# Gelu of the state-space output: on ScalarE at the end of each branch, in token order, instead of in pieces over three engines inside the attention

## The chip, the cores and the metric

One core of a Trainium2 chip runs the whole kernel. Its engines are TensorE (PE), VectorE (DVE), ScalarE (ACT), GpSimd (POOL) and SyncE (SP, which issues most of the DMAs). The metric is the device time of one execution in microseconds; of a kernel the median of several runs is given.

## What is computed

One decoder block on 1024 tokens of width 1024, 16 meta tokens ahead of them (1040 rows). An input projection gives the state-space input `u` (512 wide), q, k, v and two gates. The change touches the state-space mixer's output: an S5 scan for 32 groups of 16 channels, a gelu, and a gated linear unit. Cut from the reference:

```python
def s5_mixer(u, ...):
    ...                                   # complex diagonal scan, states s_re, s_im
    y = (jnp.einsum('blgp,gcp->blgc', s_re, c_re) - jnp.einsum('blgp,gcp->blgc', s_im, c_im)
         + d * ug)
    y = jax.nn.gelu(y.reshape(bsz, seq_len, SSM_WIDTH)).astype(u.dtype)
    return y * jax.nn.sigmoid(y @ glu_w + glu_b)

def reference(...):
    ...
    y_ssm = s5_mixer(u, ...)
    o = diff_attention(q, k, v, lam, slopes)
    mixed = sigmoid(g_ssm) * (y_ssm @ w_ssm_out) + sigmoid(g_att) * (y_att @ w_att_out)
    h = h + mixed @ w_o
    h = h + conv_glu_ffn(rmsnorm(h, norm2_g), w_up, conv_w, conv_b, w_down)
```

## The kernel before

All activations lie with channels on the 128 partitions and tokens along the free dimension. Matmuls are made exact enough by splitting each operand into a rounded part and a rest (`whi`, `wlo` of a weight, `yhi`, `ylo` of y), so that each product is three matmuls; a split is a copy on ACT and a subtract on DVE or, from the fourth gate on, a subtract on POOL.

**State-space part** (about 60 to 280 us). The 512 channels are four branches of 128. Each goes through inflow, scan, back and outflow; `ssm` is a generator that yields between the steps, and other projections are placed between them. The outflow's matmuls go to PSUM, ACT copies them to SBUF (`Vs<-yps`), and one DMA writes them to DRAM as `d_y[b]`. In this form the partitions hold position-within-a-chunk and channel, and the free dimension group and chunk: not token order. The tail of this part, from 232 us, has the last branch's steps with the first gate projections (`PRE`) between them.

**Attention** (about 290 to 640 us). Scores of a block are computed in two or three pieces of up to 512 columns: PE makes two matmuls (lines 1419 and 1420), DVE adds the bias, takes the row maximum and moves the piece to SBUF (line 1421), then a negated maximum `nm`, an exponential on ACT (`S<-S,nm`), a combination of the two softmaxes on DVE (`S<-S,c`), a transpose on PE (`wt`) copied back by ACT, and the product with v (`po`). Score pieces rotate through few PSUM tiles, so PE's next piece needs DVE to have emptied an earlier one. PE's gaps between these are filled by a generator `fillers`: first the 16 gate projections (`gates`, each three tiles of 48 matmuls, evicted by DVE as `gate<-ps_mm,R`, a tanh on ACT, then a store to `d_gate[i]` by SP), then the state-space glu and its output projection (`glu_and_out`). PE's order in the attention is the program's; the order on the other engines is made by a scheduler from its own estimate of times.

**The gelu.** When gate 14 is begun (`YGATE`), `load_y` reads the four branches back from `d_y` with 32 DMAs of 65 KB on SP, in pieces of 520 bytes, into four tiles `yt` of 128 x 8 x 130 (position in chunk, chunk). The gelu is in eight pieces of 128 x 520: the square on POOL, two multiply-adds on DVE and a tanh on ACT between them; the result is twice the gelu. During gate 15, after every sixth filler step, `split_y` splits one `yt` into `yhi` (ACT) and `ylo` (DVE), with a factor 0.5, and turns it into token order by a strided write. In `glu_and_out`, the multiply-add with `yt` reads it strided, and the split takes a factor 0.25.

**Buffers.** The tiles `gate`, `yt`, `y2`, `u` and several others share one tag `t` of five buffers: whoever takes a buffer waits for the last reader of the tile that had it.

## Time and profile before

| | us |
|---|---|
| median of three runs | 1437.9 (1436.21, 1437.9, 1437.98) |
| the profiled execution | 1438.99 |
| its span in the profile | 1437.2 |
| PE busy | 1407.9 (98%) |
| DVE busy | 1051.0 (73%) |
| ACT busy | 630.8 (44%) |
| POOL busy | 379.7 (26%) |
| granted clock of PE, mean | 0.993 |

Times in the views are counted from the span's start. A timeline's row gives start, length, engine, line, operation, output and input tile, and in brackets how long the engine had been idle before it and what ended that. `s` is a PSUM tile of scores, `S` its copy in SBUF, `ps_mm` a PSUM tile of a projection. The granted clock of a stretch is 1.00 at 2.4 GHz and 0.50 at 1.2 GHz. The line numbers are those of the kernel before; in the changed one, line 1421 is line 1429, and 446 is 452.

### The profile page before, as it was taken

Reading aid. Unit: us, or ns where it says so; the run is one execution under the profiler, and the core shown is the slowest. Engines: PE = TensorE matmul, PEld = TensorE weight load, DVE = VectorE, ACT = ScalarE, POOL = GpSimd, SP = SyncE. Lnnn points to the kernel's source line nnn. Section 1 sums busy time; section 2 is a strip of 40 time slices with the busy share of each in tenths; the row PEclk is TensorE's granted clock in tenths of the full one; section 3 lists DMA queues with packets and bytes.
Section 4 is the critical chain, followed back from the end, with each engine's and each line's share of the span. In section 5 each row is a group of like instructions: output and inputs, shape, how many; then the busy total and the mean of one; then the engine's idle time right before and its main releaser. Section 6 shows DMA issues by size and latency. Waiting matters only on the chain.

```text
span 1437.2 us, 22951 instructions
## 1 busy us (share of the span) xinstructions
PE 1407.9 (98%) x8714; PEld 1298.4 (90%) x8714; DVE 1051.0 (73%) x2030; ACT 630.8 (44%) x1180; POOL 379.7 (26%) x250
## 2 busy tenths in 40 slices
PE   8999999999998999999999999999999999999998
PEld 7999999999998999889998999988889997788887
DVE  7999996345646978548366998888766769896574
ACT  6255554345544766433254543333333333444442
POOL 2000000121111311000221156766655567131030
PEclk9999999999999999999999999999999999999999
DMA  5433343362434425656433223333323337944331
GB/s 199 137 76 115 105 122 98 111 189 60 116 102 109 115 75 185 197 191 220 133 132 114 93 81 125 126 125 117 111 97 110 111 110 258 360 150 154 123 119 58
DMA packets 93053, 191.45 MB, mean 133 GB/s; under 512 B 27536, under 2 KB 36880, under 8 KB 92944
## 3 DMA queue, kind: packets, MB, share of 16 engines
q1 hardware_dynamic: 92944, 190.00, 41.0%
q8 instruction: 68, 1.11, 0.3%
q14 instruction: 41, 0.34, 0.1%
HBM read 133.28 MB, written 55.50 MB: 131 GB/s over the span
## 4 chain that ended last, share of the span: by engine, by line
PE 76%; DVE 10%; DMA 5%; POOL 4%; issue 3%; ACT 2%; SPq 1%; DVEq 0%; ACTq 0%; POOLq 0%
PE ps_mm L184 38%; PE ps_mm L132 28%; PE po L1455 3%; DMA wraw<-in_w_up 2%; DVE wop L94 2%; POOL crow L94 2%; DVE crow L103 1%; PE s L1419 1%; PE wt L1464 1%; PE s L1420 1%; PE qss L371 1%; POOL S L94 1%; DVE u L94 1%; DMA wd<-in_w_down 1%; DMA yt<-d_y 1%
## 5 line engine op out<-in xcount | busy, mean ns | idle before, releaser
L132 PE MATMUL ps_mm<-B,wop 128*128 128x512 f32 (+2 forms) x2772 | 436.6, 319 | 4.3 <-DVE u L94 3.4
L132 PEld LDWEIGHTS ps_mm<-B,wop 128*128 128x128 f32 x2772 | 395.2, 189 | 45.3 <-ACT wop L106 5.2
L184 PE MATMUL ps_mm<-bop,wop 128*128 128x512 f32 x924 | 216.0, 395 | 2.6 <-DVE bop L94 2.6
L184 PEld LDWEIGHTS ps_mm<-bop,wop 128*128 128x128 f32 x924 | 174.1, 189 | 44.4 <-DVE bop L94 3.5
L184 PE MATMUL ps_mm<-hhi,whi 128*128 128x342 f32 (+2 forms) x432 | 138.0, 330 | 1.9 <-ACT hhi L106 1.9
L184 PE MATMUL ps_mm<-hlo,whi 128*128 128x342 f32 (+2 forms) x432 | 139.6, 323 | 0.1
L184 PE MATMUL ps_mm<-hhi,wlo 128*128 128x342 f32 (+2 forms) x432 | 139.5, 324 | 0.0
L106 ACT ACTIVATE whi<-wraw 128x1024 fp32r<-128x1024 f32 (+3 forms) x62 | 62.1, 1003 | 133.2 <-PE ps_mm L184 53.6
L94 DVE TENSOR_TENSOR wop<-wraw,wop 128x512 fp32r<-128x512 f32 x88 | 98.0, 1119 | 23.6 <-ACT wop L106 23.2
L132 PE MATMUL ps_mm<-hhi,whi 128*128 128x348 f32 (+3 forms) x336 | 111.9, 333 | 0.2 <-ACT rms_u L106 0.2
L132 PE MATMUL ps_mm<-hhi,wlo 128*128 128x348 f32 (+3 forms) x336 | 109.7, 326 | 0.0
L132 PE MATMUL ps_mm<-hlo,whi 128*128 128x348 f32 (+3 forms) x336 | 108.8, 324 | 0.0
L94 POOL TENSOR_TENSOR wlo<-wraw,whi 128x1024 fp32r<-128x1024 f32 x18 | 44.6, 2477 | 214.1 <-ACT whi L106 211.9
L94 DVE TENSOR_TENSOR wop<-S,wop 128x512 fp32r<-128x512 f32 x66 | 64.9, 983 | 48.1 <-ACT wop L106 48.1
L106 ACT ACTIVATE bop<-act 128x512 fp32r<-128x512 f32 x77 | 48.4, 632 | 117.3 <-PE ps_mm L184 117.3
L1421 DVE CUSTOM_DVE_ANT_0 S<-s,bias 128x348 f32<-128x348 f32 (+9 forms) x120 | 57.7, 483 | 56.6 <-PE s L1420 56.0
L94 POOL TENSOR_TENSOR crow<-crow,T 128x512 f32<-128x512 f32 x44 | 70.6, 1618 | 96.3 <-DVE T L94 90.8
L106 ACT ACTIVATE wop<-wraw 128x512 fp32r<-128x512 f32 x88 | 54.1, 626 | 93.2 <-DMA wraw<-in_w_up 51.6
L94 DVE TENSOR_TENSOR bop<-act,bop 128x512 fp32r<-128x512 f32 x77 | 60.1, 781 | 44.0 <-ACT bop L106 43.9
L106 ACT ACTIVATE wop<-S 128x512 fp32r<-128x512 f32 x66 | 40.4, 626 | 109.5 <-POOL S L94 98.8
L184 PEld LDWEIGHTS ps_mm<-hhi,whi 128*128 128x128 f32 x432 | 81.2, 190 | 3.1 <-ACT hhi L106 2.5
L184 PEld LDWEIGHTS ps_mm<-hlo,whi 128*128 128x128 f32 x432 | 83.0, 192 | 0.8 <-DVE hlo L103 0.6
(317 smaller groups left out, 3055.6 us busy)
## 6 DMA issues: line engine op xcount, KB each, us to landing
wraw<-in_w_up SPq DMA_DIRECT2D x49, 512.0 KB, 3.6
wraw<-in_w_in SPq DMA_DIRECT2D x30, 512.0 KB, 4.4
d_act<-crow SPq DMA_DIRECT2D x22, 512.0 KB, 2.9
act<-d_act SPq DMA_DIRECT2D x44, 256.0 KB, 3.7
wd<-in_w_down SPq DMA_DIRECT2D x22, 512.0 KB, 7.3
d_t<-T SPq DMA_DIRECT2D x33, 256.0 KB, 4.1
act<-d_t SPq DMA_DIRECT2D x33, 256.0 KB, 3.1
d_gate<-gate SPq DMA_DIRECT2D x16, 513.0 KB, 4.9
```

The source lines that it names most:

```text
L94: (eng or self.nc.vector).tensor_tensor(out=out, in0=in0, in1=in1, op=op)
L103: self.nc.vector.scalar_tensor_tensor(out=out, in0=in0, scalar=s, in1=in1, op0=op0, op1=op1)
L106: self.nc.scalar.activation(out, in_, func, **kw)
L132: self.nc.tensor.matmul(out=ps, lhsT=w, rhs=b, start=(i == 0), stop=(i == n - 1))
L184: self.nc.tensor.matmul(out=ps, lhsT=w, rhs=b, start=first and i == 0, stop=last and i == 2)
L371: self.nc.tensor.matmul(out=ps, lhsT=self.blk, rhs=v, start=True, stop=True)
L1419: nc.tensor.matmul(out=ps, lhsT=q, rhs=self.KH[j][:, c0m:c0m + cm], start=True, stop=False)
L1420: nc.tensor.matmul(out=ps, lhsT=q, rhs=self.KL[j][:, c0m:c0m + cm], start=False, stop=True)
L1421: nc.vector.tensor_tensor_reduce(out=s[0:M, c0:c0 + cn], in0=ps[0:M, off:off + cn], in1=self.bias[0:M, b0 + c0:b0 + c0 + cn], scale=1.0, s ...
L1455: nc.tensor.matmul(out=po[0:M], lhsT=l, rhs=rr, start=(kk == 0), stop=(kk == nb))
L1464: nc.tensor.transpose(ps[:, r], w[:, NM + 128 * kk:NM + 128 * (kk + 1)], b.ident)
```

## The change

Branch 3's gelu is made by the outflow's evictions on ACT (the function Gelu in place of Copy), so `d_y[3]` holds the gelu already. For branches 0 to 2, `load_branch` reads `d_y` back in the tail of the state-space part (24 small DMAs on SP), `gelu_y` makes one activation of 128 x 8 x 130 on ACT with a strided write into token order, and ACT's own queue stores it to a new `d_g[i]`. The table with Gelu (and Tanh) is loaded by a pinned preload in that tail; before, the table with Tanh was loaded just ahead of the first gate's tanh. The exponential's table is loaded once more ahead of the attention's first exponential. `load_y` then reads three contiguous tiles of 128 x 1040 from `d_g`, and branch 3 raw, which ACT copies into token order. The split of y is contiguous and without a factor (so a plain subtract on DVE), the multiply-add of the glu is contiguous, and the factor behind it is 0.5.

```diff
--- before.py
+++ after.py
@@ -47,7 +47,7 @@
 YGATE = 14
 GAP_V = 1.5
 NEWTON, NORM_SCALE = (1.0, -2.0, 16.0), -8192.0
-GELU_CUTS = 2
+GELU = "gelu_apprx_tanh_and_others"
 LN_EXP = "natural_log_exp_and_others"
 TCARGS = {"schedule_with_timeline_sim": True}
 
@@ -211,6 +211,7 @@
             self.d_gate = [d(f"d_gate{i}", [128, T2]) for i in range(16)]
             self.d_u = [d(f"d_u{i}", [GB, 16, CH, NJ]) for i in range(4)]
             self.d_y = [d(f"d_y{i}", [CH, 16, GB, NJ]) for i in range(4)]
+            self.d_g = [d(f"d_g{i}", [128, T]) for i in range(3)]
             self.d_m1 = [d(f"d_m1{i}", [128, T2]) for i in range(8)]
             self.d_o = [d(f"d_o{i}", [128, T2]) for i in range(H)]
             self.d_h2 = [d(f"d_h2{i}", [128, SEQ]) for i in range(8)]
@@ -238,7 +239,12 @@
                 step(1)
                 self.v_block(h)
             fill = self.fillers()
-            for _ in ssm:
+            tc.keep_in_program_order(nc.scalar.preload_act_table_set(GELU))
+            loaded = []
+            for n, _ in enumerate(ssm):
+                for z in loaded:
+                    self.gelu_y(*z)
+                loaded = [(i, self.load_branch(i)) for i in ((0, 1), (2,), ())[min(n, 2)]]
                 spent = 0.0
                 while spent < PRE:
                     spent += next(fill)
@@ -729,7 +735,7 @@
                                          rhs=d["Vv"][:, g0 + g], start=True, stop=False))
                     nc.tensor.matmul(out=ps[:, g], lhsT=toe[:, g0 + g].rearrange("p n c -> p (n c)"),
                                      rhs=u[:, g0 + g], start=False, stop=True)
-                self.act(y[:, g0:g0 + ng], ps, AF.Copy)
+                self.act(y[:, g0:g0 + ng], ps, AF.Copy if b < 3 else AF.Gelu_apprx_tanh)
             nc.sync.dma_start(out=self.d_y[b].rearrange("n c g j -> (n c) g j"), in_=y)
             self.tap(f"y{b}", y.rearrange("p g j -> p (g j)"))
             st[b] = None
@@ -770,27 +776,30 @@
     def load_y(self):
         self.yt, self.yh, self.yl = [], [], []
         for i in range(4):
-            t = self.tmp.tile([128, CH, NJ], F32, tag="t", name="yt")
-            for g in range(GB):
-                self.nc.sync.dma_start(out=t[g * 16:(g + 1) * 16],
-                                       in_=self.d_y[i][:, :, g, :].rearrange("n c j -> c n j"))
+            t = self.row(name="yt")
+            if i < 3:
+                self.nc.sync.dma_start(out=t, in_=self.d_g[i])
+            else:
+                self.act(t.rearrange("p (j n) -> p n j", n=CH), self.load_branch(i), AF.Copy)
             self.yt.append(t)
 
-        z = self.rowp.tile([128, CH, NJ], F32, tag="R", name="yz")
-        n = CH // GELU_CUTS
-        for i in range(4 * GELU_CUTS):
-            y = self.yt[i // GELU_CUTS][:, i % GELU_CUTS * n:(i % GELU_CUTS + 1) * n]
-            t = z[:, i % GELU_CUTS * n:(i % GELU_CUTS + 1) * n]
-            self.tt(t, y, y, ALU.mult, eng=self.nc.gpsimd)
-            self.stt(t, t, 1 / 0.044715, y, ALU.add, ALU.mult)
-            self.act(t, t, AF.Tanh, scale=0.044715 * (2 / np.pi) ** 0.5)
-            self.stt(y, t, 1.0, y, ALU.add, ALU.mult)
+    def load_branch(self, i):
+        t = self.tmp.tile([128, CH, NJ], F32, tag="t", name="yraw")
+        for g in range(GB):
+            self.nc.sync.dma_start(out=t[g * 16:(g + 1) * 16], in_=self.d_y[i][:, :, g, :].rearrange("n c j -> c n j"))
+        return t
+
+    def gelu_y(self, i, t):
+
+        o = self.row(name="yg")
+        self.tc.keep_in_program_order(self.nc.scalar.activation(o.rearrange("p (j n) -> p n j", n=CH), t,
+                                                                AF.Gelu_apprx_tanh))
+        self.nc.scalar.dma_start(out=self.d_g[i], in_=o)
 
     def split_y(self, i):
         hi = self.A.tile([128, T], F32R, tag="A", name="yhi")
         lo = self.A.tile([128, T], F32R, tag="A", name="ylo")
-        pv = lambda z: z.rearrange("p (j n) -> p n j", n=CH)
-        self.split(self.yt[i], pv(hi), pv(lo), 0.5)
+        self.split(self.yt[i], hi, lo)
         self.yh.append(hi)
         self.yl.append(lo)
 
@@ -813,9 +822,8 @@
                                                                yh[k][:, cs], yl[k][:, cs]) for k in range(4)])])
                 th = y2[:, cs]
                 self.act(th, ps, AF.Tanh, scale=0.5, bias=self.glub[:, m:m + 1])
-                self.stt(th.rearrange("p (j n) -> p j n", n=CH), th.rearrange("p (j n) -> p j n", n=CH), 1.0,
-                         yt[m][:, :, c0 // CH:(c0 + cn) // CH].rearrange("p n j -> p j n"), ALU.add, ALU.mult)
-                self.split(th, hi[:, cs], lo[:, cs], 0.25)
+                self.stt(th, th, 1.0, yt[m][:, cs], ALU.add, ALU.mult)
+                self.split(th, hi[:, cs], lo[:, cs], 0.5)
             self.tap(f"y2{m}", y2[:, 8:])
             y2h.append(hi)
             y2l.append(lo)
```

PE's order is the same before and after. What moves on the other engines:

DVE, in the attention, from the eviction of a score piece (`S,m<-s,bias`) of the block whose scores run at 456 us before. Before, with the pieces of the gelu between the evictions:

```order
L1421 ISA S,m_5114<-s,bias 128x348
L1421 ISA m_5114 128x1
L103 SCALAR_TENSOR_TENSOR yz<-yz,yt 128x520
L1421 ISA S,m_5114<-s,bias 128x344
L1421 ISA m_5114 128x1
L103 SCALAR_TENSOR_TENSOR yz<-yz,yt 128x520
L1430 TENSOR_REDUCE nm<-m_5114 128x1
L103 SCALAR_TENSOR_TENSOR yt<-yz,yt 128x520
L1421 ISA S,m_5152<-s,bias 128x348
L1421 ISA m_5152 128x1
```

and now:

```order
L1429 ISA S,m_5154<-s,bias 128x348
L1429 ISA m_5154 128x1
L1429 ISA S,m_5154<-s,bias 128x344
L1429 ISA m_5154 128x1
L1438 TENSOR_REDUCE nm<-m_5154 128x1
L98 TENSOR_SCALAR nm<-nm 128x1
L1429 ISA S,m_5192<-s,bias 128x348
L1429 ISA m_5192 128x1
L1429 ISA S,m_5192<-s,bias 128x348
L1429 ISA m_5192 128x1
```

The pieces `yz` and `yt` are gone; the evictions of the score pieces follow one another, with the block's maximum between.

ACT, in the tail of the state-space part (`Vs<-Vv` is the swap after the last branch's scan, `gate` the tanh of the first two gates). Before:

```order
L106 ACTIVATE Vs<-Vv 64x4x129 x4
L106 ACT_TABLE_LOAD
L106 ACTIVATE gate<-gate 128x1026
L106 ACTIVATE whi<-wraw 128x1024
L106 ACTIVATE gate<-gate 128x1026
L106 ACTIVATE Vs<-yps 128x390 x2
```

and now:

```order
L106 ACTIVATE Vs<-Vv 64x4x129 x4
L795 ACTIVATE yg<-yraw 128x8x130
L106 ACTIVATE gate<-gate 128x1026
L797 DMA d_g_116<-yg 128x1040
L795 ACTIVATE yg<-yraw 128x8x130
L797 DMA d_g_117<-yg 128x1040
L795 ACTIVATE yg<-yraw 128x8x130
L106 ACTIVATE whi<-wraw 128x1024
L106 ACTIVATE gate<-gate 128x1026
L797 DMA d_g_118<-yg 128x1040
L106 ACTIVATE Vs<-yps 128x390 x2
```

Three gelus and three stores issued by ACT stand among the tanhs and the weight splits; the table load is no longer here but stands nine rows earlier, ahead of the copy `whi<-wraw` that stood at 240.78 us.

ACT, in the attention, from the split of a weight and the tanh of gate 13 on (`O`, `junk` take the attention's output from PSUM, `wt` copies transposed weights). Before:

```order
L106 ACTIVATE whi<-wraw 128x1024
L106 ACTIVATE gate<-gate 128x1026
L106 ACTIVATE yz<-yz 128x520
L106 ACTIVATE O<-po 128x128
L106 ACTIVATE junk,oss<-po 128x128
L106 ACTIVATE wt<-wt 128x512
L106 ACTIVATE yz<-yz 128x520
L106 ACTIVATE S,z_5263<-S,nm 128x1040
L106 ACTIVATE wt<-wt 16x128
L106 ACTIVATE yz<-yz 128x520
L106 ACTIVATE S,Z0s<-S,nm 128x144
L106 ACTIVATE yz<-yz 128x520
```

and now:

```order
L106 ACTIVATE whi<-wraw 128x1024
L106 ACTIVATE gate<-gate 128x1026
L106 ACTIVATE S,z_5251<-S,nm 128x1040
L106 ACTIVATE O<-po 128x128
L106 ACTIVATE junk,oss<-po 128x128
L106 ACTIVATE wt<-wt 128x512
L106 ACTIVATE wt<-wt 16x128
L106 ACTIVATE yt<-yraw 128x8x130
L106 ACTIVATE S,Z0s<-S,nm 128x144
L106 ACTIVATE S,z_5324<-S,nm 128x144
```

The pieces of the tanh `yz` are gone, and one copy `yt<-yraw` of branch 3 stands between the transposes' copies and the exponentials of the next block. Its target has the buffer that gate 13's tile had, and its source has the buffer that gate 14's tile gets; on DVE the first eviction of gate 14 (`gate<-ps_mm,R`) stands between the next block's scores:

```order
L103 SCALAR_TENSOR_TENSOR S<-S,c 128x1040
L1429 ISA S,m_5294<-s,bias 128x144
L1429 ISA m_5294 128x1
L98 TENSOR_SCALAR nm<-m_5294 128x1
L94 TENSOR_TENSOR gate<-ps_mm,R 128x342
L1429 ISA S,m_5309<-s,bias 128x144
L1429 ISA m_5309 128x1
L98 TENSOR_SCALAR nm<-m_5309 128x1
```

The strided `ylo` and glu multiply-adds keep their places on DVE, in contiguous form; POOL loses its eight squares.

## Rows read from the trace of the kernel before

**Rows 1.** The page: busy us (share of the span) xinstructions.
```profile
PE 1407.9 (98%) x8714; PEld 1298.4 (90%) x8714; DVE 1051.0 (73%) x2030; ACT 630.8 (44%) x1180; POOL 379.7 (26%) x250
```

**Rows 2.** PE's waits, 440 to 520: engine, line, releaser; us, times, longest.
```profile
PE s L1419 <- DVE m L1421: 4.1, 1, 4.1
PE ps_mm L184 <- DVE gate L94: 2.1, 1, 2.1
```

**Rows 3.** Stages: PE, PEld, DVE, ACT, POOL busy; clock, DMA, GB/s.
```profile
464.00:469.34 5.34, 5.34 (x19) 5.12 (x19) 5.34 (x14) 4.39 (x7) 3.40 (x3) 0.50 0.63 114
506.89:510.30 3.41, 3.41 (x14) 3.40 (x13) 0.95 (x3) 0.65 (x5) 1.13 (x1) 0.50 0.67 195
1014.00:1020.00 6.00, 4.57 (x29) 3.97 (x28) 3.90 (x9) 1.78 (x3) 4.22 (x3) 1.00 0.18 52
1227.10:1230.50 3.40, 3.40 (x8) 2.72 (x9) 3.40 (x5) 0.00 (x0) 1.06 (x1) 0.50 0.85 266
```

**Rows 4.** Timeline of PE, three places: start, length, [idle before <-releaser].
```profile
457.34 0.32 PE L1420 MATMUL s<-KL,QQ 128*128 128x344 f32 x1
...
1017.60 0.47 PE L132 MATMUL ps_mm<-B,wop 128*128 128x512 f32 x1 [1.43 <-DVE u L94]
...
1227.08 0.79 PE L184 MATMUL ps_mm<-bop,wop 128*128 128x512 f32 x1 [2.01 <-DVE bop L94]
```

**Rows 5.** Timeline of DVE behind its first wait for yt.
```profile
461.98 1.53 DVE L103 SCALAR_TENSOR_TENSOR yz<-yz,yt 128x520 f32<-128x520 f32 x1 [4.91 <-POOL yz L94]
463.43 0.50 DVE L1421 CUSTOM_DVE_ANT_0 S<-s,bias 128x344 f32<-128x344 f32 x1
```

**Rows 6.** Timeline of POOL, its first squares.
```profile
460.89 2.06 POOL L94 TENSOR_TENSOR yz<-yt 128x520 f32<-128x520 f32 x2 [7.95 <-DMA yt<-d_y]
```

**Rows 7.** Timeline of SP: issues of the yt loads.
```profile
451.34 15.82 SPq L775 DMA_DIRECT2D yt<-d_y  x25
```

**Rows 8.** Timeline of DVE, 490 to 506: ylo and the last gate's evictions.
```profile
493.10 6.64 DVE L103 SCALAR_TENSOR_TENSOR ylo<-yt,yhi 128x1040 fp32r<-128x1040 f32 x3
...
504.38 1.35 DVE L94 TENSOR_TENSOR gate<-ps_mm,R 128x342 f32<-128x342 f32 x3
```

**Rows 9.** Groups by shape: xcount | busy us, mean ns | idle before <-releaser.
```profile
L106 ACT ACTIVATE yhi<-yt 128x1040 fp32r<-128x1040 f32 x4 | 9.0, 2306 | 0.0
...
L106 ACT ACTIVATE crow<-crow 128x1024 f32<-128x1024 f32 x22 | 23.3, 1058 | 22.2 <-DVE crow L103 22.2
...
L94 DVE TENSOR_TENSOR wlo<-wraw,whi 128x1024 fp32r<-128x1024 f32 x38 | 46.3, 1219 | 7.5 <-ACT whi L106 7.5
...
L103 DVE SCALAR_TENSOR_TENSOR ylo<-yt,yhi 128x1040 fp32r<-128x1040 f32 x4 | 8.9, 2291 | 0.0
```

**Rows 10.** Timeline of ACT in the tail of the state-space part.
```profile
240.78 1.06 ACT L106 ACTIVATE whi<-wraw 128x1024 fp32r<-128x1024 f32 x1 [1.55 <-PE ps_mm L132]
...
257.65 1.28 ACT L106 ACT_TABLE_LOAD   x1
...
258.94 1.06 ACT L106 ACTIVATE gate<-gate 128x1026 f32<-128x1026 f32 x1
```

**Rows 11.** Timeline of DVE and PE there.
```profile
258.81 0.51 DVE L94 TENSOR_TENSOR gate<-ps_mm,R 128x342 f32<-128x342 f32 x1
...
269.02 0.32 PE L184 MATMUL ps_mm<-hhi,whi 128*128 128x342 f32 x1
...
273.75 0.38 PE L728 MATMUL yps<-Vv,CL 128*128 128x130 f32 x2
```

**Rows 12.** Timeline of ACT behind the attention's first exponential.
```profile
317.24 1.06 ACT L106 ACTIVATE whi<-wraw 128x1024 fp32r<-128x1024 f32 x1 [1.88 <-issue]
```

**Rows 13.** ACT's gate13 tanh; landing of d_gate stores; PE's score matmul near 478.
```profile
467.87 1.05 ACT L106 ACTIVATE gate<-gate 128x1026 f32<-128x1026 f32 x1
...
DMA to landing us min/median/max: 3.5/4.7/8.2
...
477.95 0.37 PE L1419 MATMUL s<-KH,QQ 128*128 128x456 f32 x1
```

## The prediction

> **What bounds the kernel now.** I read the page's busy line first: TensorE (PE) is busy 98% of the span, the vector engine (DVE) 73%, ScalarE (ACT) 44% [rows 1]. So work that leaves DVE, ACT or GpSimd (POOL) is worth nothing by itself; it pays only where PE stands still for it, or where PE runs slowly after it stood still. The second view is the list of what PE waited for in the attention stretch that holds the pieces of the gelu. It has two entries of size: 4.1 us for an attention score matmul that waits for DVE, and 2.1 us for a glu matmul that waits for the last gate's eviction on DVE [rows 2]. The third view is the stage table with the granted clock: behind each of these pauses a stretch stands at clock 0.50, the lower of the two levels (1.2 instead of 2.4 GHz). It lasts to 469.34 after the first and for 3.41 us after the second [rows 3]. The same happens behind the pause of 2.01 us before 1227.08, and does not behind the pause of 1.43 us before 1017.60 [rows 3, 4]. So I charge a new pause with a slow stretch where it is as long as those that had one (2.01 and more), and with none where it is as short as the one that had none.
>
> Then I follow each pause to its cause. **First pause.** DVE executes in order. It sat idle 4.91 us before its first piece of the gelu at 461.98, waiting for POOL's square [rows 5]; POOL had itself sat 7.95 us until 460.89, waiting for the load of yt [rows 6]; SP was busy for 15.82 us issuing 25 of the 32 small loads [rows 7]. The score eviction that PE needed stood behind that piece, and ran at 463.43 [rows 5]. PE restarted at 464.00, where the slow stretch of [rows 3] begins for it. **Second pause.** Four strided ylo of 2.29 us each stand on DVE [rows 9]; three took 493.10 to 499.74, and the gate's evictions came only at 504.38 [rows 8].
>
> What the two are worth, if they vanish entirely: 4.1 us of standing [rows 2], plus half of the 5.34 us that PE worked at half clock (464.00 to 469.34 [rows 3]), 2.7, is 6.8. Then 2.1 plus half of 3.41, 1.7, is 3.8. Together 10.6.
>
> **What the change removes there.** All eight squares on POOL and all sixteen DVE pieces, so nothing on DVE waits for yt any more before the score evictions. The score eviction that ran at 463.43 had its matmul done by 457.66 [rows 4], so DVE can run it then: the first pause goes completely, and with it the slow clock. Costs in its place: ACT now does S exp, weight split, gate tanh, and an output eviction with less spread. I allow 0.15 for a transpose's copy that comes late.
>
> For the second pause ylo becomes one contiguous subtract instead of a strided piece. The nearest row is the contiguous subtract of 128x1024, 1.219 us against 2.291 [rows 9]. Four of them save 4.3 us of DVE before the gate's evictions, where PE was missing 2.1, and the DVE time of the gelu pieces ahead of them has gone too. So some 2 us of slack are left and the 3.8 comes back. The strided multiply-adds of the glu get shorter as well, but no pause of any size hangs on them: nothing.
>
> **What the change adds, and what hides it.**
> (a) Branch 3's gelu rides on its outflow evictions in place of a copy: nothing, as a function's cost does not show in the rows (gelu in the feed-forward part, 128x1024, takes 1.058 [rows 9], gate tanh, 128x1026, 1.05 [rows 13]).
> (b) In the tail of the state-space part, 24 small loads on SP, three gelus on ACT, three stores issued from ACT's own queue. SP is moved first: eleven loads ahead of the Toeplitz loads, at some 0.6 us of issue each by 15.82/25 [rows 7], so these come about 7 us later; PE reads their tile only in the outflow that begins at 273.75 [rows 11], some 30 us on. Nothing. A strided gelu costs 2.31 us by the strided yhi, which is the nearest row, or 1.06 by the contiguous gelu [rows 9]; I take 2.31. ACT's queue by rows: the table load that stood at 257.65 [rows 10] is moved forward into idle time of 1.55 us before 240.78 [rows 10], where its 1.28 fits. The first gelu takes 257.65 to 259.96, gate0's tanh ends at 261.0, the second gelu at about 263.4 (a store's issue between them, 0 to 0.6). DVE's gate1 eviction at 258.81 [rows 11] writes the buffer that the second gelu reads, so it now waits till about 263.6, and what is queued behind it on DVE, the scan's product Vv, with it. PE wants the gate's tile in PSUM free at 269.02 and Vv at 273.75 [rows 11]: 5 us and more of cover. The third gelu waits for its loads and for the first store's landing, and is done by about 272.6; the weight split and gate1's tanh behind it come 7 us late, and no matmul before 290 uses those weights. Nothing again.
> (c) ACT's table must be changed back before the first exponential of the attention: one more load, 1.28 us by the row at 257.65. If it comes in whole behind the wait of that exponential, ACT still idles 1.88 us behind the exponential, before 317.24 [rows 12], which absorbs it. Nothing.
>
> The Trainium skill, page "ScalarE: Activation LUTs", section "What ACT_TABLE_LOAD costs", speaks against (c): a load costs about 1.28 us and a drain of about 1.38 with it, 2.66 for each change of set. In the trace the next activation starts at 258.94, 1.29 after the load's start, so the row carries the load and no drain behind it. By the page the exponential would start up to 2.66 us late, of which 1.88 is absorbed, and 0.8 would fall on the weight split at 317.24; the sum would not move by more than that.
>
> (d) **The new wait.** Branch 3's y is loaded raw and copied on ACT into token order, strided, 2.31 us by yhi [rows 9]. Its target buffer was that of gate13, so the copy must wait until gate13's store has landed. This is a wait that before did not have. Gate13's tanh ran at 467.87 [rows 13], 3.87 us after PE's restart, most of it at half clock. With PE running on from 459.86 at full clock I estimate the tanh at 462.1 and its store issued at 463.2. Stores of gates land 3.5 to 8.2 us after issue, median 4.7 [rows 13]: 467.9, at worst 471.4. ACT is blocked until then, with two exponentials of 128x144 and an output eviction queued behind the copy. DVE's first eviction of gate14 needs the raw buffer and waits for the copy's end, about 470.2; two score evictions stand behind it. PE's next score matmul (477.95 before [rows 13]; 477.95 − 6.8 = 471.15 now) needs the first of them: 470.2 + 0.5 for the gate eviction + 0.3 to 0.5 for the score eviction is 471.0 to 471.2. At the median landing the wait just touches PE, and the next score, 1.6 us on, some tenths more. Every us by which the landing is later costs PE one, and a long pause the slow clock as well. So 0 at the low end, 3.5 + 1.7 at the high end; I take 1.0, as the wait is nearest to the median row.
>
> **Sum.** 10.6 − 0.15 − 1.0 = 9.5 us. The profiled execution took 1438.99 (span 1437.2, so 1.8 lie around the span and do not change); its median sibling 1437.9. The sum comes from waits of one execution and I subtract it from the median: 1437.9 − 9.5 = 1428.4.
>
> **The rivals.**
> *The copy's wait grows to 2 us and more.* For it: the store's landing was 8.2 us once [rows 13], and two loads of q and k rows now stand directly ahead of it in SP's queue. Against: these loads are due long before 463. Price: 2.5 of pause + 1.7 of slow clock instead of 1.0, gain 6.4: 1431.5.
> *The second pause stays.* For it: the copy delays everything on DVE before the splits, and branch 3's split is the last of four. Against: 4.3 us less of ylo. Price: only the first pause pays, 6.8 − 1.15 = 5.65: 1432.3; half of it gone, about 1430.
> *The copy costs little.* If its strided write cost what the contiguous gelu costs, 1.058 us instead of 2.306 [rows 9], it would end 1.25 us earlier and PE would not wait: gain 10.5, 1427.4. Against: yhi is the same write, with another output type. The Trainium skill, same page and section, gives an activation 0.19 us plus 0.833 ns per element of a partition, 1.05 us for 1040, and names no layout; the contiguous row agrees, yhi does not, so I hold to yhi.
> *Nothing is gained.* DVE turns out to be late at 460 to 464 for another reason than the yt load, for instance as ACT's exponentials feed it late. Against: the score eviction has its input from 457.7 on, and DVE was idle. Price: 1437 to 1439.
> *Slower, by the state-space tail.* The second gelu holds DVE at gate1's first eviction. It decides from the point where that gelu ends after 268.5 (269.02 less an eviction of 0.5): each us beyond costs PE one, and a long pause another 1.7 for the clock. To eat the 9.5 and more it would have to end at 280, 16 us past my estimate; the gelus would have to take 10 us each, where no row shows more than 2.5 for one pass of 1040 elements on ACT, or the raw loads land 16 us late. Price: 1441 to 1444.
>
> **How the numbers follow.** Both pauses gone, with a wait at the copy of under 2 us: 0.60, of it 0.15 for the cheap copy; 1426.5 to 1429.4. Copy's wait of 2 us and more: 0.16, 1430 to 1432.5. Second pause stays or stays in part: 0.13, 1430 to 1432.3. Nothing gained: 0.05. Slower: 0.04. More than the two pauses (the small ones at 479, 489, 549 and 552, together 0.9, go too): 0.02, down to 1426.4. Bounds: gain 10.6 + 0.9 and a run 0.9 lower than the sum give 1425.5; the two rivals and a run 0.5 higher give 1432.8. Range 1425.5 to 1432.8. This kernel's measurement tells apart about 0.2%, 2.9 us: faster means under 1435.0, slower over 1440.8. Faster 0.91, same 0.05, slower 0.04.
>
> **What would show it.** In the waits of PE between 440 and 520 both entries should be gone, and the stage table should stand at clock 1.00 from 455 to 515. If a pause of PE stands near 471 to 473, with DVE's gate eviction behind ACT's copy, (d) is right, and its length gives the mis-sizing. ACT should show the copy with idle time ahead of it that ends with the landing of gate13's store. A strided gelu of 2.3 us near 258, DVE idle at gate1's first eviction until about 263.6, and no pause of PE from 255 to 280 confirm (b); a pause there is the slower case. A table load of 1.28 before the attention's first exponential and no pause after it confirm (c). The prediction is wrong if the clock is not 1.00 after 460 though no pause is left, or if a pause at 459.9 stays without any yt piece ahead of the score eviction.

## The result and the profile after

The changed kernel takes 1431.0 us (median of 5 runs, 1429.1 to 1434.1), against 1437.9 before. The ratio is 0.9949, with a 95% interval of 0.9931 to 0.9968: a gain of 7.3 us by that ratio, 4.6 to 9.9 by the interval. Measured once more in another session (a0 below) it is 0.9944 [0.9928, 0.9959]. The forecast was 1428.4 in a range of 1425.5 to 1432.8, and faster with 0.91. It is faster by over 0.2%, the time lies in the range, 2.6 us above the forecast.

The page's busy line of after, with the columns of [rows 1]:

```profile
PE 1404.2 (98%) x8714; PEld 1295.4 (91%) x8714; DVE 1029.2 (72%) x2014; ACT 631.9 (44%) x1177; POOL 371.8 (26%) x242
```

PE's busy share is 98% as before. Its busy time fell by 3.7 us, where the profiled span fell by 8.0 (1437.2 to 1429.2), so this line shows less than half of the gain. PE's waits show more: both entries of [rows 2] are gone in the stretch 440 to 520. What stands there instead is new.

```profile
PE s L1427 <- DVE m L1429: 1.1, 2, 0.6
```

To lay two kernels side by side I cut the stretch around the change at four instructions of PE that both have. The first cut is a matmul of a gate projection, 4.7 us ahead of the old first pause; the last is 150 us on, in the attention. The length of each piece is then the time from one instruction to the same instruction. The first two of the four pieces of before (columns as in [rows 3]: stretch, its length, busy us of PE, PEld, DVE, ACT, POOL, granted clock, DMA share, GB/s):

```profile
455.12:481.04 25.92, 21.68 (x123) 20.19 (x121) 19.84 (x46) 10.80 (x25) 12.05 (x9) 0.87 0.71 168
481.04:512.11 31.07, 28.67 (x180) 26.82 (x178) 25.56 (x56) 22.48 (x36) 5.55 (x5) 0.95 0.35 102
...
```

And of after, between the same instructions:

```profile
456.58:477.02 20.44, 19.33 (x123) 18.02 (x121) 10.70 (x41) 9.61 (x21) 2.37 (x1) 1.00 0.66 178
477.02:503.59 26.57, 26.57 (x179) 25.31 (x178) 17.38 (x45) 16.49 (x34) 6.31 (x4) 1.00 0.33 102
...
```

Piece 1 holds the old first pause and the new copy, piece 2 the old second pause. They are 5.5 and 4.5 us shorter and the clock stands at 1.00 in both, where before had 0.87 and 0.95. The four together went from 149.9 to 139.8: 10.1 us. The work that PE does is the same; what went is the standing still and the matmuls at half clock.

The same cut was made in every kernel. All lengths in us; "outside" is the span less the four pieces:

| kernel | piece 1 | piece 2 | piece 3 | piece 4 | sum | outside | median us | ratio to before [95%] |
|---|---|---|---|---|---|---|---|---|
| before | 25.92 | 31.07 | 72.91 | 20.01 | 149.9 | 1287.3 | 1437.9 | |
| b0 before, once more | 25.70 | 31.05 | 72.94 | 20.12 | 149.8 | 1290.1 | 1441.7, one run | |
| after | 20.44 | 26.57 | 72.11 | 20.69 | 139.8 | 1289.4 | 1431.0 | 0.9949 [0.9931, 0.9968] |
| a0 after, once more | 21.34 | 26.58 | 72.12 | 20.72 | 140.8 | 1287.6 | 1431.4 | 0.9944 [0.9928, 0.9959] |
| e1 contiguous copy | 20.27 | 26.58 | 72.61 | 20.24 | 139.7 | 1289.0 | 1430.5 | 0.9940 [0.9924, 0.9957] |
| e2 two copies | 22.09 | 26.58 | 72.13 | 22.37 | 143.2 | 1289.2 | 1434.8 | 0.9965 [0.9953, 0.9976] |
| e6 branch 3 early | 18.79 | 26.58 | 72.25 | 22.60 | 140.2 | 1290.9 | 1431.9 | 0.9945 [0.9927, 0.9963] |
| e3 strided split | 22.97 | 28.56 | 72.11 | 22.81 | 146.5 | 1290.3 | 1434.6 | 0.9957 [0.9940, 0.9974] |
| e7 no gelu pieces | 22.54 | 27.78 | 73.30 | 20.36 | 144.0 | 1289.3 | 1434.1 | 0.9963 [0.9950, 0.9975] |
| e4 four loads | 23.24 | 28.77 | 72.92 | 20.13 | 145.1 | 1286.3 | 1436.3 | 0.9979 [0.9965, 0.9992] |
| e5 three gelus | 20.87 | 26.58 | 72.11 | 22.59 | 142.2 | 1293.2 | 1435.8 | 0.9976 [0.9962, 0.9990] |
| e8 early and orow | 18.79 | 26.58 | 71.93 | 17.84 | 135.1 | 1294.6 | 1427.6 | 0.9920 [0.9901, 0.9938] |
| e9 orow alone | 21.32 | 26.58 | 72.12 | 17.60 | 137.6 | 1287.1 | 1427.0 | 0.9916 [0.9900, 0.9932] |

Two executions of one code differ by 0.1 to 1.0 us inside the four pieces and by 1.8 to 2.8 outside. So the pieces tell apart what the medians only bound. A profile is of one run, not of the median one: those of e3, e7 and e8 are of the slowest run of their kernel, that of e4 of the second fastest of ten. The ratios are to runs of before in the same session (a0, e1, e2 and e6 shared one; e3, e4 and e7 another; e5, e8 and e9 a third).

### The profile page after: what moved, and what is told of

Read it like the earlier page. It is cut to its first block, busy times and chain, and to the rows that moved or that the text cites. A ratio compares the mean times of both kernels' runs of the same rounds, so it can differ in the third digit from the quotient of the medians.

```text
span 1429.2 us, 22918 instructions
## 1 busy us (share of the span) xinstructions
PE 1404.2 (98%) x8714; PEld 1295.4 (91%) x8714; DVE 1029.2 (72%) x2014; ACT 631.9 (44%) x1177; POOL 371.8 (26%) x242
## 3 DMA queue, kind: packets, MB, share of 16 engines
q8 instruction: 68, 1.11, 0.3%
## 4 chain that ended last, share of the span: by engine, by line
PE 88%; DVE 6%; DMA 3%; issue 1%; ACT 1%; POOL 1%; SPq 0%; ACTq 0%; DVEq 0%; POOLq 0%
PE ps_mm L184 40%; PE ps_mm L132 37%; PE po L1463 3%; DVE wop L94 1%; PE s L1427 1%; PE wt L1472 1%; PE s L1428 1%; PE qss L377 1%; DMA wraw<-in_w_up 1%; DMA wd<-in_w_down 1%; PE vps L694 1%; PE yps L736 1%; PE yps L734 0%; PE km L672 0%; DVE crow L103 0%
```

## The experiments

Edits are against the changed kernel, or against before where that is said.

**The changed kernel once more (a0).** 

> The changed kernel once more, for its own spread and as the base of the others. By the sum of waits: both pauses of the kernel before gone, two pauses of together 1.1 us behind the copy of branch 3's y, and the rest of the 9.5 us lost elsewhere only by chance (the first 42 us of the profiled execution took 1.3 longer than before, ahead of anything that the change touches). Then the time is 1429 to 1431 and the pause of 1.87 us near 592 (0.60 before) is seen again or not by chance. Rival: the changed kernel is slower at the start or near 592 by its order; then both stand in this profile as well.

It measured 0.9944, as the first time. The copy waits for the store of gate13, and here the trace names it (ACT's timeline):

```profile
462.92 1.04 ACT L106 ACTIVATE gate<-gate 128x1026 f32<-128x1026 f32 x1
...
470.72 2.20 ACT L106 ACTIVATE yt<-yraw 128x1040 f32<-128x1040 f32 x1 [3.85 <-DMA d_gate<-gate]
```

PE's pauses behind it are 1.50 and 0.52 us, against 0.60 and 0.51 in the first profile of after. Nothing in the code differs; the landing was 1.0 us later after the store's issue (6.7 against 5.7).

**A cheaper copy (e1)**

```
-  self.act(t.rearrange("p (j n) -> p n j", n=CH), self.load_branch(i), AF.Copy)
+  self.act(t.rearrange("p (n j) -> p n j", n=CH), self.load_branch(i), AF.Copy)
```

> The changed kernel with the copy of branch 3's y written contiguously (so its glu input stands in the wrong token order). By my step (d): the copy takes about 1.06 instead of 2.25 us, the chain copy, gate eviction, score eviction ends 1.2 earlier, the two pauses near 473 and 475 (0.60 and 0.51) vanish, 0.9 to 1.1 us faster than the changed kernel. Rival (the layout does not set an activation's cost): the copy still takes 2.25 and nothing changes.

ACT's timeline of e1:

```profile
469.75 1.08 ACT L106 ACTIVATE yt<-yraw 128x1040 f32<-128x1040 f32 x1 [3.90 <-DMA d_gate<-gate]
```

The copy takes 1.08 instead of 2.25 us, so the layout of the write makes its price. Piece 1 is 0.2 to 1.1 us shorter than in the two runs of after, and pauses of 0.43 and 0.52 are left. The time, 0.9940, can't be told from a0. The store lands so late (6.5 us after its issue here) that even a copy of half the length touches PE.

**The copy twice (e2)**

```
-  self.act(t.rearrange("p (j n) -> p n j", n=CH), self.load_branch(i), AF.Copy)
+  raw = self.load_branch(i)
+  for _ in range(2):
+      self.act(t.rearrange("p (j n) -> p n j", n=CH), raw, AF.Copy)
```

> The changed kernel with that copy made twice, 2.25 us more on ACT. By my step (d) PE's pauses near 473 grow by 2.25, from 1.1 to about 3.4, and a stretch at half clock follows, 1.7 more: 3 to 4.5 us slower than the changed kernel. Rival (DVE and PE have cover there): under 1 us slower.

PE's timeline at the copy:

```profile
477.73 0.48 PE L1429 MATMUL s<-KH,QQ 128*128 128x456 f32 x1 [3.04 <-DVE m L1431]
```

And the stage behind it:

```profile
477.80:485.00 7.20, 7.20 (x46) 6.68 (x47) 5.80 (x24) 4.47 (x10) 0.11 (x1) 1.00 0.01 2
```

Counted from the first cut the copies end at 470.67 + 4.45 − 457.10 = 18.0, in a0 at 470.72 + 2.20 − 456.00 = 16.9. PE stands 3.04 us against 2.02 in a0. The copies end 1.1 us later and PE stands 1.0 us longer: the chain from landing over copy and gate eviction to the score is real. But no half clock follows a pause of 3.04 us. The median is 3.3 us above a0's; 0.75 of it stands in piece 1 of the profiles and 1.65 in piece 4, of which more below. So the time falls in the expected range, but not for the expected reason: the half clock that was to make up 1.7 of it did not come at the copy, and in this profile the loss in piece 4 took its place.

**Branch 3 earlier, without the wait (e6).** Its raw load and copy go ahead of gates 5 and 7, it is stored in token order, and the attention loads it as it does the other three.

```
+  if i == 5:
+      raw = self.load_branch(3)
+  if i == 7:
+      o = self.row(name="yg")
+      self.act(o.rearrange("p (j n) -> p n j", n=CH), raw, AF.Copy)
+      self.nc.sync.dma_start(out=self.d_g[3], in_=o)
...
-  if i < 3: ...
-  else: self.act(t.rearrange("p (j n) -> p n j", n=CH), self.load_branch(i), AF.Copy)
+  self.nc.sync.dma_start(out=t, in_=self.d_g[i])
```

> The changed kernel with branch 3 read back raw at gate 5, copied into token order at gate 7 and stored to a fourth d_g, so that all four yt are contiguous loads and no copy waits for gate 13's store. By my step (d): pauses near 473 gone, none new between 300 and 440 (PE had none there), 0.9 to 1.1 us faster than the changed kernel. Rival: the copy blocks ACT near 320, where it has only 0.6 us idle, ahead of two exponentials, and PE waits there for 1 to 2 us: same or slower.

The stages of e6, pieces 1 and 4:

```profile
455.60:474.39 18.79, 18.79 (x121) 18.03 (x121) 11.01 (x41) 8.24 (x21) 2.37 (x1) 1.00 0.65 200
...
573.22:595.82 22.60, 19.69 (x117) 18.49 (x116) 12.46 (x32) 9.94 (x22) 0.00 (x0) 0.92 0.67 194
```

The rival's wait near 320 did not come: PE has none from 240 to 440. In piece 1 PE is busy without a gap at clock 1.00, so I take 18.79 us as its floor. So the first pause was worth 25.8 − 18.8 = 7.0 us, and the copy costs 20.44 − 18.79 = 1.65 or, in a0, 2.55. Yet the time is a0's. In the profile 1.9 us of the gain are lost again in piece 4, at clock 0.92.

**Before, once more (b0).** 

> The kernel before once more, for a second look at pauses that the change doesn't touch. By my reading the pauses of 4.1 and 2.1 us near 460 and 503 with their slow stretches stand again, within 0.5 us; the pause or pauses of together 1.85 us near 592 to 601, which hang on a chain of two DMAs, vary by a us, as in the changed kernel (2.54, 2.54, 2.11 us in three looks at it and at the contiguous copy); the first 42 us vary too. Rival: they stand within 0.2 us of the first look; then what the changed kernel lost there comes from the change.

The first pause is 3.90 us and half clock follows it for 3.42 us, where [rows 3] had 4.1 and 5.34. Piece 1 differs by only 0.2, since a second pause of 0.96 us, before 480.35, stands in it that the first profile did not have.

**Before, without the pieces of the gelu (e7).** 

> The kernel before without its gelu in the attention (left out altogether; the 32 loads and the strided splits stay). By the sum: the first pause and its slow stretch go, 6.8 us; no copy, so no pause near 473; the second pause stays in part, 1 to 2.3 us with or without 1.7: gain over the kernel before 7 to 9 us, 1429 to 1431. Rival (the second pause came from the pieces): both gone, gain 10.6 and more, 1427.

The gain is 5.3 us by the ratio, less than the 7 to 9 expected. The old first pause is gone, and another stands further on (it ends 18.2 us from the first cut, the old one 8.9). SP, DVE and PE of e7, in order of time:

```profile
454.15 14.57 SPq L775 DMA_DIRECT2D yt<-d_y  x24
468.82 0.38 SPq L446 DMA_DIRECT2D d_gate<-gate  x1
...
475.32 0.52 DVE L94 TENSOR_TENSOR gate<-ps_mm,R 128x342 f32<-128x342 f32 x1 [5.20 <-DMA d_gate<-gate]
...
476.11 0.47 PE L1410 MATMUL s<-KH,QQ 128*128 128x456 f32 x1 [1.93 <-DVE m L1412]
...
476.70 0.49 PE L184 MATMUL ps_mm<-hhi,whi 128*128 128x342 f32 x1
...
480.00 0.32 PE L184 MATMUL ps_mm<-hhi,whi 128*128 128x342 f32 x1
```

Gate13's store stands on SP behind 24 small loads of yt; gate14's first eviction needs a buffer that this store has to free, and the score eviction queues behind it. So with the pieces gone the small loads cost PE time by themselves, in front of gate13's store. In before they did not hold it: the pause had made gate13's tanh so late (it ended at 468.92) that the store went out right behind it, at 468.95. In the changed kernel most of these loads are gone from in front of the store, but the copy has joined the wait for its landing.

**Before, with four loads of yt in place of 32 (e4)**

```
-  for g in range(GB):
-      self.nc.sync.dma_start(out=t[g * 16:(g + 1) * 16], in_=self.d_y[i][:, :, g, :].rearrange("n c j -> c n j"))
+  self.nc.sync.dma_start(out=t.rearrange("p n j -> p (n j)"), in_=self.d_y[i].rearrange("n c g j -> (n c) (g j)"))
```

> The kernel before with yt loaded by four contiguous DMAs of 532 KB instead of 32 small ones (so the tiles hold the values of d_y in another order; all the rest of the gelu stays, in the order that the scheduler makes of it). By my reading of the first pause, the loads that land late: DVE does not wait for yt at 457 to 462 any more, the first pause goes with its slow stretch, the second stays: gain 5 to 7 us, 1431 to 1433. Rival (the pieces themselves, in DVE's order, hold the score evictions): a pause of 1 to 3 us stays between 457 and 485, gain under 4.

DVE and PE of e4, in order of time:

```profile
456.86 1.53 DVE L103 SCALAR_TENSOR_TENSOR yz<-yz,yt 128x520 f32<-128x520 f32 x1 [0.95 <-POOL yz L94]
...
458.89 0.42 PE L1418 MATMUL s<-KH,QQ 128*128 128x344 f32 x1 [1.04 <-DVE m L1420]
...
466.18 2.76 DVE L103 SCALAR_TENSOR_TENSOR yt<-yz,yt 128x520 f32<-128x520 f32 x1
...
469.49 1.16 PE L1454 MATMUL po<-Vt,wt 128*128 128x128 f32 x8 [1.63 <-ACT wt L106]
...
501.99 0.43 PE L184 MATMUL ps_mm<-yhi,whi 128*128 128x344 f32 x1 [1.85 <-DVE gate L94]
```

With the data there in time, DVE's wait of 4.91 us [rows 5] shrinks to 0.95 and PE's 4.1 to 1.04. But PE stands 1.63 from 467.86 to 469.49, where DVE works off its pieces (two of them in a row at 466.18, 2.76 us) and ACT has its own. Piece 1 gains 2.6 of the 7.0. The late load explains the old first pause as it stood; with it mended the pieces would still cost most of it. So the rival held, also in the time: 0.9979 is a gain of 3.0 us where I had 5 to 7. The pieces of this profile show 4.8, but it is of one of the fastest runs.

**The changed kernel with before's strided split (e3)**

```
-  self.split(self.yt[i], hi, lo)
+  pv = lambda z: z.rearrange("p (j n) -> p n j", n=CH)
+  self.split(pv(self.yt[i]), pv(hi), pv(lo))
```

> The changed kernel with only the split of y strided again (read and written in the old pattern, the same values). By my reading of the second pause, four strided ylo on DVE: yhi and ylo take 2.2 to 2.3 us each again, the gate's evictions are ready 1 to 2.3 us after PE needs them, so a pause of 1 to 2.3 us near 498, with or without a slow stretch of 1.7: 1 to 4 us slower than the changed kernel. Rival (the second pause came from the gelu pieces ahead of the splits): no pause near 498, same time.

DVE's ylo of e3, and the last gate's evictions:

```profile
488.85 4.73 DVE L94 TENSOR_TENSOR ylo<-yt,yhi 128x1040 fp32r<-128x1040 f32 x2 [2.28 <-ACT yhi L106]
493.95 2.61 DVE L94 TENSOR_TENSOR ylo<-yt,yhi 128x1040 fp32r<-128x1040 f32 x1 [0.37 <-ACT yhi L106]
...
501.29 0.93 DVE L94 TENSOR_TENSOR gate<-ps_mm,R 128x342 f32<-128x342 f32 x2
```

In after a ylo takes 1.24 us, two of the four somewhat more, and these evictions stand at 497.76. The strided ylo are back at 2.3 to 2.6 us and piece 2 is 2.0 longer than in after, with pauses of 0.89 and 0.55. But the old pause of 2.1 with its half clock does not come back. Piece 1 is longer as well: the pause at the copy is 2.24 here, to 474.46, and the piece's clock is 0.93. So of the 3.2 us that the median lies above a0's (1.9 by the two ratios, whose intervals overlap) not all belongs to the split. The 2.0 us and the two pauses are read from one profile, of the slowest run.

**Three passes of the gelu in the tail of the state-space part (e5)**

```
+  for _ in range(3 if i < 2 else 1):
       self.tc.keep_in_program_order(self.nc.scalar.activation(o.rearrange("p (j n) -> p n j", n=CH), t, ...
```

> The changed kernel with each of the first two gelus in the state-space tail made three times. By my step (b): the second branch's gelu ends near 274 instead of 264.4, DVE's gate1 eviction starts there, and PE, which needs that tile of PSUM at about 270.5 (269.02 plus the 1.46 by which this stretch came later in the changed kernel), stands for 3.5 to 4.5 us; with a slow stretch 1.7 more: 4 to 6 us slower than the changed kernel. Rival (the tail has more cover than I gave it): no pause between 255 and 285, same time.

PE doesn't pause between 255 and 285. It pauses 30 us later, with half clock behind. ACT, DVE and PE of e5:

```profile
262.36 4.53 ACT L796 ACTIVATE yg<-yraw 128x1040 f32<-128x1040 f32 x2
...
266.96 0.94 DVE L94 TENSOR_TENSOR gate<-ps_mm,R 128x342 f32<-128x342 f32 x2 [6.37 <-PE ps_mm L184]
274.46 0.93 DVE L94 TENSOR_TENSOR gate<-ps_mm,R 128x342 f32<-128x342 f32 x2 [3.73 <-ACT yg L796]
...
302.88 0.43 PE L184 MATMUL ps_mm<-hhi,whi 128*128 128x342 f32 x1 [1.93 <-DVE gate L94]
...
303.46 0.49 PE L184 MATMUL ps_mm<-hhi,whi 128*128 128x342 f32 x1
```

Gate 0's last eviction stands at 257.51, so the two at 266.96 are gate 1's first ones. They came right behind the third pass of the first branch's gelu (262.36 + 4.53 = 266.89), not behind the second branch's at 274.42, and so before the 270.5 at which PE was to need them; the two at 274.46 are gate 2's. The deadline in my step (b) was therefore not put to the test. What was late is another chain. The loads of q and k for the attention wait for the store of `d_y`'s last branch to land. They went out at 286.31 instead of 283.72, and behind them K, Q, a weight split and a gate's evictions on DVE came some 2.5 us late, the evictions at 302.31. The store itself was issued at 279.82 against 279.39 in after, but landed 6.4 us later instead of 4.2; the third store of a gelu now goes out 1.6 us ahead of it (278.26, in after 271.40). That this makes it late is argued, not shown. The time is 4.4 above a0's, in the expected range but not for the expected reason. So the tail has room for the gelus as they are, and where it runs out is not where I looked.

**Piece 4 (e8 and e9).** Piece 4 holds none of the changed code, but it is 2 to 3 us longer in e2, e3, e5 and e6 than in before. PE waits there for a score eviction that stands on DVE behind the split of orow, a row of the attention's output. Its load waits on SP until the store d_m has landed, since both use one buffer. SP, ACT and PE of before, in order of time:

```profile
582.10 0.32 SPq L834 DMA_DIRECT2D d_m<-g1row  x1
...
586.00 0.32 SPq L895 DMA_DIRECT2D orow<-d_o  x1
...
590.93 1.06 ACT L106 ACTIVATE ohi<-orow 128x1026 fp32r<-128x1026 f32 x1 [2.95 <-DMA orow<-d_o]
...
593.79 0.44 PE L1419 MATMUL s<-KH,QQ 128*128 128x392 f32 x1 [1.25 <-DVE m L1421]
```

The same in e6:

```profile
570.29 0.32 SPq L845 DMA_DIRECT2D d_m<-g1row  x1
...
575.29 0.32 SPq L906 DMA_DIRECT2D orow<-d_o  x1
...
580.73 1.06 ACT L106 ACTIVATE ohi<-orow 128x1026 fp32r<-128x1026 f32 x1 [4.54 <-DMA orow<-d_o]
...
583.59 0.48 PE L1430 MATMUL s<-KH,QQ 128*128 128x392 f32 x1 [2.84 <-DVE m L1432]
```

From d_m's issue to orow's it is 3.90 us in before and 5.00 in e6; the pause grows from 1.25 to 2.84, and the clock falls. In e2, e3 and e5 the two issues are 5.39, 5.33 and 5.06 us apart, in after and a0 4.12 and 4.57: the kernels with the long piece 4 are those where the store landed late. Why it did so in them stays open. The edit gives this row a buffer of the group R, where the gelu's scratch yz stood in before and which is free at this time. (In before it is free by then too: the last piece of the gelu starts at 485.5. The same edit was not run there.)

```
-  o = self.row(n=T2, name="orow2")
+  o = (self.rowp.tile([128, T], F32, tag="R", name="orow2")[:, 0:T2] if h == 0 else
+       self.row(n=T2, name="orow2"))
```

e8 is e6 with this edit, e9 the changed kernel with it. 

> The changed kernel with branch 3 read back and turned into token order at gates 5 and 7 (as before in e6), and in addition the first of the reloaded attention rows put into the buffer of the row pool, which the gelu's scratch tile held before the change, so that its load does not wait for the store of a merged row to land. By the reading of e6: no pause between 440 and 540, and the pause of 2.8 us near 581 with its slow stretch gone or under 1: 1426 to 1429. Rival (that pause hangs on the chain of score and DVE work, not on the load): the pause near 581 stays, 1430 to 1432.

> The changed kernel with only the first of the reloaded attention rows in the buffer of the row pool. The pauses of together 1.1 to 2 us near 473 stay, the ones near 584 to 592 (2.5 together) shrink to under 1: 1 to 2 us faster than the changed kernel, 1429 to 1430. Rival: the pauses there stay.

SP of e9:

```profile
573.69 0.32 SPq L842 DMA_DIRECT2D d_m<-g1row  x1
574.06 0.43 SPq L904 DMA_DIRECT2D orow<-d_o  x1
```

And its piece 4:

```profile
576.62:594.22 17.60, 17.60 (x117) 16.95 (x116) 10.70 (x27) 9.60 (x21) 0.00 (x0) 1.00 0.74 234
```

The load goes out 0.37 us after the store, PE has no gap, and piece 4 is 17.6 instead of 20.7. Both medians, 1427.6 and 1427.0, lie some 4 us below the changed kernel's (for e9 that is 2 us more than expected), and the slowest run of e9, 1428.3, is below the fastest of the changed kernel, 1429.1. e8 removes 2.5 us more in the four pieces, but its median shows nothing of that; its profile is of its slowest run and the longest of all outside the pieces, and which of the two is the better stays open. Of e9's 4 us, 2.2 to 3.1 stand in the four pieces; the rest is not located.

## Why the prediction was right, and where it was off

**Both pauses are gone: right.** The first was worth 7.0 us by e6's floor; the forecast had 6.8. The clock is 1.00 behind it.

**The second pause: right in size, short in its reason.** Piece 2 went from 31.06 to 26.58, 4.5 us against 3.8. I put it down to the ylo in the main. With the pieces out and the strided split kept, e3 loses 2.0 of the 4.5 and e7 1.2. So, with the pieces taken out first, 2.5 to 3.3 us came from the pieces and 1.2 to 2.0 from the contiguous split. The other order, the split contiguous and the pieces kept, was not run; the shares could come out otherwise there. The pieces' time on DVE and ACT ahead of the splits was named in the prediction as a by-product; in this order it was the larger part.

**The new wait (d): the place was right, its landing was the term mis-sized.** SP, ACT and DVE of after, in order of time:

```profile
462.18 0.34 SPq L1353 DMA_DIRECT2D qkvrow<-d_qkv  x1
462.62 1.09 SPq L1358 DMA_DIRECT2D qkvrow<-d_qkv  x2
...
463.50 1.04 ACT L106 ACTIVATE gate<-gate 128x1026 f32<-128x1026 f32 x1
...
464.56 0.34 SPq L452 DMA_DIRECT2D d_gate<-gate  x1
...
470.34 2.25 ACT L106 ACTIVATE yt<-yraw 128x1040 f32<-128x1040 f32 x1 [2.89 <-DMA wraw<-in_w_ssm_out]
...
472.62 0.52 DVE L94 TENSOR_TENSOR gate<-ps_mm,R 128x342 f32<-128x342 f32 x1 [3.86 <-ACT yt L106]
473.06 0.30 DVE L1429 CUSTOM_DVE_ANT_0 S<-s,bias 128x144 f32<-128x144 f32 x1
```

Everything stands in the order forecast: tanh, store, landing, copy, gate eviction, score eviction, PE. The store's issue fits: forecast 463.2, and the stretch begins 1.46 us later here (456.58 against 455.12). The strided copy is 2.25 long against 2.31. But from the store's issue to the copy's start it is 5.8 us, in a0 6.7, in e1 6.6, in e2 5.6, where I took the median 4.7. The reason that I had set aside is the likely one: the prediction held that the loads of q and k "are due long before 463", and three of them (it counted two) stand right ahead of the store, issued 462.18 to 463.71. Where they do not, the store lands sooner. SP of e6, and the landing of this one store (the last figure of the row, us from its issue) in after and in e6:

```profile
455.90 1.69 SPq L1361 DMA_DIRECT2D qkvrow<-d_qkv  x2
463.58 0.33 SPq L458 DMA_DIRECT2D d_gate<-gate  x1
...
d_gate<-gate SPq DMA_DIRECT2D x1, 513.0 KB, 5.7
...
d_gate<-gate SPq DMA_DIRECT2D x1, 513.0 KB, 4.4
```

In the seven kernels with the loads just ahead (after, a0, e1, e2, e3, e5, e9) it lands 5.5 to 6.7 us after its issue; in e4, e6 and e8, where they had gone out about 6 us or more before it, after 4.4 to 4.8. These edits changed other traffic too, so this speaks strongly for the three loads and does not single them out. (The trace names another DMA as the copy's releaser in the first profile, a weight load issued 1.5 us after the store; but the store's landing, 464.56 + 5.7 = 470.3, is just when the copy starts, and in a0 and e1 it names the store.) So the copy costs 1.65 to 2.55 where I had 1.15. With the pauses at 1.11 to 2.02 together, the run lies between my likeliest case and the rival of a wait of 2 us and more; no half clock followed either, so the 1.7 that the rival added did not come.

**The cheap copy as a rival.** The Trainium skill, page "ScalarE: Activation LUTs", section "What ACT_TABLE_LOAD costs", gives figures for an activation that make 1.05 us for 1040 elements, an estimate, and names no layout. e1 shows 1.08 for the contiguous write, and after 2.25 for the same elements written with a stride; the rows decide for the stride, as I had chosen. The Trainium skill, page "SBUF — State Buffer", section "Door 1: The DMA port swizzle", names a reason that would fit: each access that crosses to a new 16-byte line of SBUF pays a penalty. The strided write steps by 8 elements of 4 bytes. The rows show the price, not the reason. The rival falls in its result too: even at 1.08 a pause of 0.95 is left.

**The tail of the state-space part (b): right.** ACT and DVE of after, beside [rows 10, 11]:

```profile
259.11 2.29 ACT L795 ACTIVATE yg<-yraw 128x1040 f32<-128x1040 f32 x1
...
262.16 2.23 ACT L795 ACTIVATE yg<-yraw 128x1040 f32<-128x1040 f32 x1
...
264.43 0.93 DVE L94 TENSOR_TENSOR gate<-ps_mm,R 128x342 f32<-128x342 f32 x2 [4.08 <-DMA d_g<-yg]
```

And the stage:

```profile
240.00:300.00 60.00, 60.00 (x396) 60.00 (x396) 28.19 (x41) 28.96 (x34) 6.08 (x9) 1.00 0.61 182
```

The second gelu ends at 264.4 (forecast 263.4, and the stretch begins 1.46 us later here), the gate's eviction follows at 264.43 (263.6), and PE is busy for all 60 us. (The trace names the first gelu's store as what released the eviction, but that landed 3.9 us after its issue at 261.43; in e2, e3 and e9 it names the gelu.) The slower rival put its point of decision at this eviction, at 268.5; in e5 it came at 266.96, short of that point, and the tail gave way elsewhere.

**Branch 3's gelu on its evictions (a): right.** The evictions `Vs<-yps` of 128x390 take 495 ns in the mean of all eight in both kernels, so the gelu in two of them costs nothing.

**The table load (c): right.** Before the first exponential of the attention stands

```profile
315.54 1.28 ACT L106 ACT_TABLE_LOAD   x1 [3.59 <-DVE nm L98]
316.83 1.17 ACT L106 ACTIVATE S<-S,nm 128x1040 f32<-128x1040 f32 x1
```

The exponential starts 1.29 us after the load, so of the drain of about 1.38 us that the Trainium skill adds (page "ScalarE: Activation LUTs", section "What ACT_TABLE_LOAD costs") nothing is seen here either. PE does not pause from 300 to 440.

**The sum.** The waits were to give 9.5 us; the four pieces give 10.1 and, in a0 against b0, 9.1. This agreement is in part luck, as misses of both signs offset each other: the second pause gave 0.7 more, the copy took 0.5 to 1.4 more, piece 4 lost 0.6 to 0.7, and piece 3 gave 0.8 that the sum had at nothing. Piece 3 is 72.9 to 73.3 us long in the four kernels with the strided multiply-adds of the glu (before, b0, e4, e7) and 71.9 to 72.6 in the nine with the contiguous ones (1.05 and 0.77 us each on DVE), of which the prediction said that no pause of any size hangs on them. The medians give 7.3 and 8.1 by the two ratios, with 9.5 inside both intervals. Outside the pieces the two profiles of before average 1288.7 and the two of after 1288.5: no loss is to be seen there, but executions of one code differ there by up to 2.8 us, and a us or two could hide in that. The 2.6 us between forecast and median are not settled beyond that.

## What to carry to other kernels

Moving work off an engine that isn't the bound pays where the bound waits for it or runs slowly after the wait: count both, from one instruction to the same instruction in both kernels. When a step is moved next to a store that must land first, look at what the DMA queue issues just ahead of that store, and where other transfers stand there take the long landing, not the median. Look for buffers that are free when a load waits for another transfer's landing only because both use one buffer: giving such a load a free one brought 4 us, over half as much as the change.

## What was not expected of the hardware

A pause's length alone does not tell whether half clock follows. After 3.04 us (e2, to 477.73) the clock stayed at 1.00, after 1.95 (a0, to 585.52) and 1.85 (e4, to 501.99) too; after 1.93 (e7, to 476.11, and e5, to 302.88), 2.24 (e3, to 474.46) and 2.84 (e6, piece 4 at 0.92) it fell. My rule from [rows 3, 4], that pauses of 2.01 us and more bring it, does not hold; what decides it in these runs stays open.

The store of one gate landed 5.5 to 6.7 us after its issue in the seven kernels where three loads stand right ahead of it, and 4.4 to 4.8 in the three where they went out earlier.
